# One kernel, two edits to its attention stages: float32 probabilities and values with two heads in column halves, and a second score pass in row halves

## The chip, the cores and the metric

The kernel runs on one core of a Trainium2 chip. The metric is the device time of one execution in microseconds; the time shown for a kernel is the median of its runs. TensorE multiplies, VectorE, ScalarE and GpSimd (POOL in the profile) do the elementwise work, SyncE's queue issues most transfers. TensorE's results land in PSUM, eight banks of 512 float32 columns over 128 partitions.

## What is computed

Two blocks over 1024 tokens of width 1024, all inputs and outputs in float32. The first block has two layers (a Hyena convolution mixer, then grouped-query attention), each with a cross attention to 256 memory rows and a mixture of experts; the second has a recurrent layer beside a latent attention (MLA), and a state-space layer. The change touches the three attentions only:

```python
# memory cross attention, 4 heads of 64, in both layers of the first block; and blocked_gqa: 12 query heads, 4 key heads of 64
s = einsum(q, k) / 8 ;  p = softmax(s) ;  out = einsum(p, v)
# _mla_attention: 8 heads, scores over 64 + 32 columns, values of 64, causal in blocks of queries
s = (einsum('bqhd,bkhd->bhqk', q_nope, k_nope) + einsum('bqhr,bkr->bhqk', q_rope, k_rope)) * scale
p = softmax(where(mask, s, -inf)) ;  out = einsum('bhqk,bkhd->bqhd', p, v)
```

## The kernel before

Precision is kept by splitting: a float32 operand becomes a rounded part ("hi", type fp32r, which TensorE multiplies in one pass) and the remainder ("lo", also fp32r). `Kern.split` (L130, L134) writes hi on ScalarE and lo on VectorE or POOL. A projection uses three of the four products (`mm3`).

GQA (`Gqa.attend`, L1414). Heads run one after the other. `keys` makes for a key head two tiles of 128 partitions and 1024 columns: hi twice, one above the other, and lo twice. `stack` makes for a query head one tile with hi in one half of the partitions and lo in the other (its lower half on POOL, L1411); its pool has two buffers. So one matmul over 128 rows adds two products, and `scores` (L840) needs two passes of 1024 columns per tile of 128 queries: against hi, then against lo. `exp_rows` takes the row maximum out of PSUM (VectorE, L873) and the exponential with its sum (ScalarE, L875). `pT` (L885) transposes the 128x1024 probabilities in eight blocks (TensorE, L125), four to a bank, and splits them into `gph` and `gpl`; in one of eight cases the split is done later on POOL (`pc`). After four such tiles (half of the queries), `out_heads` (L903) multiplies: the 128 weight columns are the values' hi and lo side by side, the moving operand is `gph`, then `gpl`, for each of eight key blocks; the two halves of the 128 output partitions are taken out by ScalarE and added by POOL, the reciprocal sums are brought into rows by four transposes (`columns_to_rows`) and multiplied in on POOL, and the result goes to DRAM. Of PSUM's eight banks the score tiles have 2 x 2 (`s`), the transposes 3 (`tp`), the output 1 (`ov`).

Memory attention (`Mem.attend`, L814) is the same on 256 keys with two heads in one score tile; its calls are issued between the projections of the two mixers. MLA (`mla_attend`, L1709) runs eight heads over tiles t = 4, 5, 6, 7, 0, 1, 2, 3; `mla_tile` makes scores in three passes in up to two of four one-bank tiles, `mla_pT` transposes and splits, `mla_out` multiplies, scales by the sums and a gate tile loaded from DRAM, and stores. Its probability tiles have one buffer each, for one head.

The order of the instructions on each engine isn't written out by hand. It is fixed when the kernel is built (`schedule_with_timeline_sim=True`): for each engine, as soon as it is free in a model of the run, the ready instruction that stands earliest in the program is taken. On the chip each engine then runs its list in order.

## Time and profile before

| | us |
|---|---|
| median of 3 runs | 3917.97 (3914.57 to 3920.28) |
| profiled execution | 3916.14 |
| its span in the trace | 3913.2 |
| first attention's own stage (GQA) | 1615 to 1920 of the span |
| last attention (MLA) | 2812 to 2978 |
| memory attention | within 90 to 440, and within 1500 to 1615 |

How to read the rows below: times are microseconds from the start of the span, means are ns. PE is TensorE, PEld its weight loads, DVE VectorE, ACT ScalarE. A tile is named by the program (`gs` GQA's scores, `prob` probabilities, `pT` their transposes, `ov` the product with the values; `as`, `apT`, `ao` the same in MLA; `ms` the memory's scores), a line is that of the helper that issued it. Matmuls are pipelined: the distance of two starts is what one costs in a row, its own duration is longer.

### The profile page before, as it was taken

The page shows a single profiled execution, that of the slowest core. Times are in us where ns is not written, and L with a number is a line of the kernel's source. Part 1 is how long each engine was busy: PE and PEld are TensorE (multiplying, and loading weights), DVE is VectorE, ACT ScalarE, POOL GpSimd, SP SyncE. Part 2 cuts the span into 40 slices and gives each one's busy share as a digit, 9 for nine tenths or more (in the row PEclk, how much of TensorE's full clock was granted, in tenths as well). Part 3 has the DMA queues.
Part 4 walks back from the last instruction along what each step waited for, and adds up shares of the span by engine and source line. Part 5 has one row for each costly group of instructions (what it writes and reads, how often), then busy time and mean ns, then how long its engine had stood idle before and what let it go on. Part 6 is the DMA issues. An engine that isn't in the chain of part 4 may idle for free.

```text
span 3913.2 us, 52413 instructions
## 1 busy us (share of the span) xinstructions
PE 3553.0 (91%) x19471; PEld 3025.0 (77%) x19471; DVE 2859.2 (73%) x4803; ACT 2030.9 (52%) x3047; POOL 1453.8 (37%) x1175
## 2 busy tenths in 40 slices
PE   7997999985999979899877999989998999999998
PEld 6885878764988879777767888878777877778777
DVE  6547878867988789677687988766476666665675
ACT  4433532223776754799625776645584245545430
POOL 2004745400543422244302444313451049774610
PEclk9998999897999999999988999999999999999999
DMA  4223333464999951000366999841014312222241
GB/s 159 91 82 108 116 130 116 138 212 173 363 366 346 369 166 37 11 12 12 115 242 228 386 348 345 302 136 53 33 48 131 100 48 92 71 76 85 90 171 65
DMA packets 205720, 603.61 MB, mean 154 GB/s; under 512 B 23110, under 2 KB 114104, under 8 KB 179865
## 3 DMA queue, kind: packets, MB, share of 16 engines
q1 hardware_dynamic: 193769, 558.58, 39.4%
q0 software_dynamic: 11696, 41.69, 4.1%
q8 instruction: 153, 2.51, 0.3%
q14 instruction: 102, 0.84, 0.1%
HBM read 503.60 MB, written 96.60 MB: 153 GB/s over the span
## 4 chain that ended last, share of the span: by engine, by line
PE 54%; DVE 11%; POOL 7%; ACT 4%; DMA 3%; issue 3%; SPq 0%; ACTq 0%; DVEq 0%; POOLq 0%
PE out L176 11%; PE gate L176 8%; PE xbc L176 5%; PE up L176 5%; PE down L176 4%; DVE mwl L134 4%; PE ov L176 2%; PE gs L176 2%; PE pT L125 2%; PE z L176 2%; PE as L176 1%; POOL csr L2062 1%; PE qk L176 1%; PE xr L176 1%; POOL csr L2061 1%
## 5 line engine op out<-in xcount | busy, mean ns | idle before, releaser
L134 DVE TENSOR_TENSOR mwl<-mwr,mwh 128x1024 fp32r<-128x1024 f32 x486 | 646.5, 1382 | 55.2 <-ACT mwh L130 54.3
L130 ACT ACTIVATE mwh<-mwr 128x1024 fp32r<-128x1024 f32 x576 | 563.0, 1051 | 52.5 <-PE up L176 28.8
L134 POOL TENSOR_TENSOR mwl<-mwr,mwh 128x1024 fp32r<-128x1024 f32 x90 | 257.4, 2885 | 272.2 <-ACT mwh L130 253.8
L1226 POOL DMA_INDIRECT xg<-xn_d,idx x32 | 58.8, 1838 | 466.2 <-DVE gsc L1224 465.6
L915 POOL TENSOR_TENSOR oh<-oh,oh 64x256 f32<-64x256 f32 (+1 forms) x56 | 56.0, 1000 | 396.3 <-ACT oh L914 392.1
L134 DVE TENSOR_TENSOR gpl<-pT,gph 128x512 fp32r<-128x512 f32 x168 | 110.6, 685 | 40.6 <-ACT gph L130 26.7
L1494 DVE SCALAR_TENSOR_TENSOR cv<-xbc,sdcols,cv 128x1021 f32<-128x1021 f32 (+2 forms) x72 | 91.9, 1276 | 65.3 <-ACT cv L1491 65.0
L125 PE MATMUL pT<-ident,prob 128*128 128x128 f32 x896 | 127.0, 277 | 13.6 <-DVE gpl L134 8.6
L873 DVE TENSOR_REDUCE mx<-gs 128x1 f32<-128x1024 f32 x96 | 116.9, 1218 | 30.6 <-PE gs L176 30.4
L176 PE MATMUL gate<-mwh,xgl 128*128 128x384 f32 x512 | 137.3, 349 | 0.5 <-DVE xgl L134 0.4
L125 PEld LDWEIGHTS pT<-ident,prob 128*128 128x128 f32 x896 | 106.0, 142 | 39.2 <-DVE gpl L134 6.3
L176 PE MATMUL gate<-mwl,xgh 128*128 128x384 f32 x512 | 134.6, 342 | 0.9 <-DVE mwl L134 0.8
L176 PE MATMUL gate<-mwh,xgh 128*128 128x384 f32 x512 | 134.0, 341 | 0.0
L176 PE MATMUL up<-mwl,xgh 128*128 128x384 f32 x512 | 132.0, 337 | 1.9 <-DVE mwl L134 1.9
L176 PE MATMUL out<-pwh,pyl 128*128 128x512 f32 x384 | 122.4, 400 | 11.4 <-DVE pyl L134 5.9
L176 PE MATMUL up<-mwh,xgh 128*128 128x384 f32 x512 | 132.1, 338 | 0.0
L176 PE MATMUL up<-mwh,xgl 128*128 128x384 f32 x512 | 131.6, 337 | 0.0
L130 ACT ACTIVATE xgh<-xgT 128x512 fp32r<-128x512 f32 (+1 forms) x68 | 38.1, 567 | 173.2 <-PE xgT L125 172.6
L176 PE MATMUL down<-mwl,hh 128*128 128x512 f32 x384 | 122.2, 399 | 6.1 <-POOL mwl L134 6.0
L134 DVE TENSOR_TENSOR wl<-raw,wh 128x1024 fp32r<-128x1024 f32 x71 | 109.2, 1539 | 22.6 <-ACT wh L130 22.5
L176 PE MATMUL down<-mwh,hl 128*128 128x512 f32 x384 | 122.1, 397 | 0.0
L176 PE MATMUL out<-pwh,pyh 128*128 128x512 f32 x384 | 121.2, 396 | 0.0
(753 smaller groups left out, 11725.7 us busy)
## 6 DMA issues: line engine op xcount, KB each, us to landing
mwr<-in_exp_w_gate_dram SPq DMA_DIRECT2D x64, 1536.0 KB
mwr<-in_exp_w_up_dram SPq DMA_DIRECT2D x64, 1536.0 KB
mwr<-in_exp_w_down_dram SPq DMA_DIRECT2D x64, 1536.0 KB
csr<-cs_d SPq DMA_DIRECT2D x32, 512.0 KB
raw<-in_ssd_w_in_dram SPq DMA_DIRECT2D x15, 1024.0 KB
k_d<-kev SPq DMA_DIRECT2D x54, 256.0 KB
kt<-k_d SPq DMA_DIRECT2D x54, 256.0 KB
raw<-in_hy_w_in_dram SPq DMA_DIRECT2D x10, 1024.0 KB
```

Of the source, the lines that this page charges most:

```text
L125: self.nc.tensor.transpose(out, in_, self.ident[:n, :n])
L130: nc.scalar.activation(out=hi, in_=src, func=AF.Copy)
L134: e.tensor_tensor(out=lo, in0=src, in1=hi.bitcast(F32), op=OP.subtract)
L176: self.nc.tensor.matmul(out=out, lhsT=lhsT, rhs=rhs, start=start, stop=stop)
L873: nc.vector.tensor_reduce(out=mx, in_=ps, axis=AX.X, op=OP.max, negate=True)
L915: nc.gpsimd.tensor_tensor(out=o2, in0=o2, in1=o, op=OP.add)
L1226: nc.gpsimd.indirect_dma_start(out=xg, out_offset=None, in_=self.xnD, in_offset=bass.IndirectOffsetOnAxis(ap=idx[:, 0:1], axis=0))
L1494: nc.vector.scalar_tensor_tensor(out=out[:, d:T], in0=ps[:, 0:T - d], scalar=cols[j], in1=out[:, d:T], op0=OP.mult, op1=OP.add)
L2061: G.tensor_tensor(out=m, in0=m, in1=per(self.cs[:, c, hs], P), op=OP.subtract)
L2062: G.tensor_tensor(out=m, in0=m, in1=self.msk.rearrange("p (o l) -> p o l", o=1).broadcast_to([P, 8, P]), op=OP.mult)
```

## The change

Values and probabilities stay float32. `pT` copies each bank of transposes once, to a float32 tile, by the engine that its argument names: in GQA the first four blocks by ScalarE, the last four by VectorE; in the memory attention all by ScalarE; in MLA the first bank by VectorE, the second by ScalarE. `out_pair` multiplies for two heads: head 0 writes output partitions 0 to 63, head 1 partitions 64 to 127, in turn, each with 64 weight columns (its float32 values). GQA and MLA therefore go by pairs of heads. `pair_rows` spreads the pair's reciprocal sums over 2 x 64 columns on POOL and transposes them once for both heads; the product is one VectorE instruction over 128 partitions, and one store goes out per pair. `pair_scores` makes GQA's scores for a pair: head 0's full pass against hi, then lo for both heads in row halves (64 partitions each, query hi against key lo; the product of query lo and key lo falls away), then head 1's full pass. The PSUM banks stay as they were.

```diff
@@ -814,8 +814,7 @@
     def attend(self, wk, mixT, row0, pair, qs, tg, pk=None):
         K = self.K
-        ph = wk.tile([P, 4, 256], F32R, name="mph", tag="mph")
-        pl = wk.tile([P, 4, 256], F32R, name="mpl", tag="mpl")
+        pt = wk.tile([P, 4, 256], F32, name="mpt", tag="mpt")
         for tt in range(2):
             t = tg * 2 + tt
             ps = K.psum("ms", "s")
@@ -823,11 +822,13 @@
                 h = 2 * pair + q
                 scores(K, ps[:, q * 256:(q + 1) * 256], qs[q][:, t * P:(t + 1) * P], self.k2[h], self.kl2[h])
             prob = softmax_rows(K, pk or wk, ps[:, 0:512], 2)
-            pT(K, prob, ph, pl, tt)
...
+            pT(K, prob, pt, tt, ("act",))
+        r0 = row0 + pair * P
+        ps = out_pair(K, [[pt[:, 2 * q + mb] for mb in range(2)] for q in range(2)],
+                      [[self.v[:, mb, (2 * pair + q) * 64:(2 * pair + q + 1) * 64] for mb in range(2)] for q in range(2)], "tp")
+        o = wk.tile([P, 256], F32, name="oh", tag="oh")
+        K.nc.scalar.activation(out=o, in_=ps[:, 0:256], func=AF.Copy)
+        K.nc.sync.dma_start(out=mixT.piece(r0, r0 + P, tg * 256, (tg + 1) * 256), in_=o)
 def query_stack(K, s, ps, q):
@@ -876,13 +877,37 @@
     return p
-def columns_to_rows(K, ps, v):
...
+def pair_scores(K, ps, qs, kk):
+
+
+    n = ps[0].shape[1]
+    cuts = [slice(o, min(n, o + 512)) for o in range(0, n, 512)]
+    own = [slice(0, 64), slice(64, 128)]
+    for c in cuts:
+        K.mm(ps[0][:, c], qs[0], kk[0][0][:, c], True, False)
+    for c in cuts:
+        for q in range(2):
+            K.mm(ps[q][:, c], qs[q][own[q]], kk[q][1][own[q], c], q == 1, q == 0)
+    for c in cuts:
+        K.mm(ps[1][:, c], qs[1], kk[1][0][:, c], False, True)
+
+
+def pair_rows(K, pool, sums, tag):
+
+    nc = K.nc
+    n = sums.shape[1]
+    nc.vector.reciprocal(out=sums, in_=sums)
+    b = pool.tile([P, n, 2, 64], F32, name=tag + "b", tag=tag + "b", bufs=1)
+    nc.gpsimd.tensor_copy(out=b, in_=sums.rearrange("p n (q o) -> p n q o", o=1).broadcast_to([P, n, 2, 64]))
+    rp = K.psum("rT", "tp")
+    for j in range(n):
+        K.transpose(rp[:, j * P:(j + 1) * P], b[:, j].rearrange("p q d -> p (q d)"))
+    r = pool.tile([P, n * P], F32, name=tag, tag=tag)
+    nc.scalar.activation(out=r, in_=rp[:, 0:n * P], func=AF.Copy)
+    return r
+
+
+def pT(K, prob, pt, tt, engs):
     nc = K.nc
     s = slice(tt * P, (tt + 1) * P)
@@ -891,36 +916,22 @@
         for k in range(4):
             K.transpose(ps[:, k * P:(k + 1) * P], prob[:, (h + k) * P:(h + k + 1) * P])
         v = ps[:, 0:512].rearrange("p (k t) -> p k t", k=4)
-        if h in off:
...
+        if engs[h // 4] == "act":
+            nc.scalar.activation(out=pt[:, h:h + 4, s], in_=v, func=AF.Copy)
         else:
-            K.split(ph[:, h:h + 4, s], pl[:, h:h + 4, s], v)
...
+            nc.vector.tensor_copy(out=pt[:, h:h + 4, s], in_=v)
+
+
+def out_pair(K, pt, vs, tag, cut=lambda k: 0):
+
+    n = pt[0][0].shape[1]
     ps = K.psum("ov", tag)
-    for j, (k, v) in enumerate(kv):
...
+    m = len(pt[0])
+    for k in range(m):
+        c = cut(k)
+        for q in range(2):
+            K.mm(ps[q * 64:(q + 1) * 64, c:n], vs[q][k], pt[q][k][:, c:n], k == 0, k == m - 1)
+    return ps
 NE = 16
@@ -1373,8 +1384,7 @@
         for j, (wh, wl) in enumerate(ws):
             K.mm3(ps[:, j * 256:(j + 1) * 256], lambda k: uh[:, k, ts], lambda k: ul[:, k, ts], lambda k: wh[:, k], lambda k: wl[:, k], KT, n=256)
         if u == 1:
-            p3 = ps[:, 0:256].rearrange("p (h d) -> p h d", h=4)
-            K.split(self.v[:, t, :, 0:64], self.v[:, t, :, 64:128], p3)
+            nc.scalar.activation(out=self.v[:, t], in_=ps[:, 0:256], func=AF.Copy)
             return
         x = self.rotated(wk, ps, u, t)
         tp = K.psum("qkT")
@@ -1413,23 +1423,29 @@
     def attend(self, wk, mixT, kpools, qp, op):
         K = self.K
-        for h in range(NH):
-            kv = h // 3
...
+        kk = {}
+        for pr in range(NH // 2):
+            hs = (2 * pr, 2 * pr + 1)
+            for h in hs:
+                if h // 3 not in kk:
+                    kk[h // 3] = self.keys(kpools[h // 3 % 2], h // 3)
+            qs = [self.stack(qp, h) for h in hs]
             for tg in range(2):
-                ph = wk.tile([P, 8, 512], F32R, name="gph", tag="gph")
-                pl = wk.tile([P, 8, 512], F32R, name="gpl", tag="gpl")
...
+                pt = [wk.tile([P, 8, 512], F32, name=f"gpt{q}", tag=f"gpt{q}") for q in range(2)]
+                sm = op.tile([P, 4, 2], F32, name="gsm", tag="gsm", bufs=2)
                 for tt in range(4):
                     t = tg * 4 + tt
-                    ps = K.psum("gs", "s")
-                    scores(K, ps, qs[:, t * P:(t + 1) * P], k2, kl)
...
+                    ps = [K.psum("gs", "s") for q in range(2)]
+                    pair_scores(K, ps, [s[:, t * P:(t + 1) * P] for s in qs], [kk[h // 3] for h in hs])
+                    for q in range(2):
+                        prob = exp_rows(K, wk, ps[q], sm[:, tt, q:q + 1])
+                        pT(K, prob, pt[q], tt, ("act", "dve"))
+                po = out_pair(K, [[pt[q][:, kb] for kb in range(8)] for q in range(2)],
+                              [[self.v[:, kb, h // 3 * 64:h // 3 * 64 + 64] for kb in range(8)] for h in hs], "ov")
+                r = pair_rows(K, op, sm, "orc")
+                o = op.tile([P, 512], F32, name="oh", tag="oh")
+                K.nc.vector.tensor_tensor(out=o, in0=po[:, 0:512], in1=r, op=OP.mult)
+                K.nc.sync.dma_start(out=mixT.piece(pr * P, (pr + 1) * P, tg * 512, (tg + 1) * 512), in_=o)
 ALPHA = float(np.float32(4.0 ** 0.25))
@@ -1694,7 +1710,7 @@
             v = ps.rearrange("p (h d) -> p h d", h=8)
             nc.scalar.activation(out=kf[:, :, 0:64], in_=v[:, :, 0:64], func=AF.Copy)
             nc.gpsimd.tensor_copy(out=kf[:, :, 64:96], in_=self.kr[:, t:t + 1].broadcast_to([P, 8, 32]))
-            K.split(self.v[:, t, :, 0:64], self.v[:, t, :, 64:128], v[:, :, 64:128])
+            nc.vector.tensor_copy(out=self.v[:, t], in_=v[:, :, 64:128])
             for src, dst, eng in ((qf, self.qT, "act"), (kf, self.kT, "dve")):
                 for h0 in range(0, 8, 4):
                     tp = K.psum("mT", "tp")
@@ -1720,19 +1736,19 @@
             for s in (slice(0, T),) if h else (slice(0, 512), slice(512, T)):
                 for i, x in ((2, self.kT), (0, self.qT)):
                     K.split(qk[i][:, s], qk[i + 1][:, s], x[h // 4][0:96, h % 4, s], lo_eng="pool" if h else "dve")
-            pp = []
...
+            q = h % 2
+            if q == 0:
+                pp = [[cp.tile([P, 4 + 4 * tg, 512], F32, name=f"ap{x}{tg}") for tg in range(2)] for x in range(2)]
+                sm = cp.tile([P, 2, NT, 2], F32, name="asm", tag="asm", bufs=2)
+                G.memset(sm[:, 1, 0:4], 0.0)
             todo = [4, 4]
             for t in (4, 5, 6, 7, 0, 1, 2, 3):
-                p = self.mla_tile(wk, qk, t, idb, msk, sm)
...
+                p = self.mla_tile(wk, qk, t, idb, msk, sm[:, :, :, q])
+                tg = t // 4
+                self.mla_pT(p, pp[q][tg], t)
+                todo[tg] -= 1
+                if q and not todo[tg]:
+                    self.mla_out(wk, yT, h // 2, tg, [x[tg] for x in pp], sm[:, :, 4 * tg:4 * tg + 4])
     def mla_tile(self, wk, qk, t, idb, msk, sm):
@@ -1761,42 +1777,36 @@
             nc.scalar.activation(out=p[:, o:o + w], in_=ps[:, 0:w], func=AF.Exp, bias=mx[:, 2 * m - 2:2 * m - 1], accum_out=sm[:, j, t:t + 1])
         return p
-    def mla_pT(self, p, pp, t):
...
+    def mla_pT(self, p, pt, t):
+
+        K, nc = self.K, self.K.nc
         cs = slice(t % 4 * P, (t % 4 + 1) * P)
         for k0 in range(0, t + 1, 4):
             m = min(4, t + 1 - k0)
             tp = K.psum("apT", "tp")
             for k in range(m):
                 K.transpose(tp[:, k * P:(k + 1) * P], p[:, (k0 + k) * P:(k0 + k + 1) * P])
-            K.split(ph[:, k0:k0 + m, cs], pl[:, k0:k0 + m, cs], tp[:, 0:m * P].rearrange("p (k t) -> p k t", t=P))
...
+            src = tp[:, 0:m * P].rearrange("p (k t) -> p k t", t=P)
+            if k0:
+                nc.scalar.activation(out=pt[:, k0:k0 + m, cs], in_=src, func=AF.Copy)
+            else:
+                nc.vector.tensor_copy(out=pt[:, k0:k0 + m, cs], in_=src)
+
+    def mla_out(self, wk, yT, pr, tg, pt, sm):
         K, nc = self.K, self.K.nc
-        gt = wk.tile([64, 512], F32, name="ag", tag="ag", bufs=1)
...
+        gt = wk.tile([P, 512], F32, name="ag", tag="ag", bufs=1)
+        dst = yT.piece(512 + pr * P, 512 + (pr + 1) * P, tg * 512, (tg + 1) * 512)
         nc.sync.dma_start(out=gt, in_=dst)
-        rs = K.small.tile([P, 4], F32, name="ars", tag="ars", bufs=2)
+        rs = wk.tile([P, 4, 2], F32, name="ars", tag="ars", bufs=2)
         nc.vector.tensor_tensor(out=rs, in0=sm[:, 0], in1=sm[:, 1], op=OP.add)
-        nc.vector.reciprocal(out=rs, in_=rs)
...
+        r = pair_rows(K, wk, rs, "arb")
         nc.gpsimd.tensor_tensor(out=gt, in0=r, in1=gt, op=OP.mult)
-        po = K.psum("ao", "ov")
...
+        n = tg * 4 + 4
+        po = out_pair(K, [[x[:, k] for k in range(n)] for x in pt], [[self.v[:, k, 2 * pr + q] for k in range(n)] for q in range(2)], "ov",
+                      lambda k: max(0, k - tg * 4) * P)
+        o = wk.tile([P, 512], F32, name="aoh", tag="aoh", bufs=1)
+        nc.vector.tensor_tensor(out=o, in0=po[:, 0:512], in1=gt, op=OP.mult)
         nc.sync.dma_start(out=dst, in_=o)
```

The allocations change with it: `mv`, `vst`, `mlv` hold 64 float32 columns per head (`mlv` now `[P, NT, 8, 64]`).

## Rows read from the trace of the kernel before

**Rows 1.** The page: busy time, share of the span and instructions of TensorE.

```profile
PE 3553.0 (91%) x19471; PEld 3025.0 (77%) x19471; DVE 2859.2 (73%) x4803; ACT 2030.9 (52%) x3047; POOL 1453.8 (37%) x1175
```

**Rows 2.** Busy times by stretch: memory attention twice, GQA, MLA; last columns clock, DMA.

```profile
core 0: us, PE busy (x) PEld busy (x) DVE busy (x) ACT busy (x) POOL busy (x), PEclk, DMA share, GB/s
90.00:440.00 350.00, 324.88 (x1564) 265.20 (x1563) 225.85 (x287) 144.37 (x267) 92.09 (x120) 0.95 0.28 95
...
1500.00:1615.00 115.00, 107.67 (x864) 104.08 (x863) 95.86 (x266) 64.21 (x154) 26.93 (x25) 0.98 0.09 25
1615.00:1920.00 305.00, 288.86 (x1637) 236.33 (x1636) 225.18 (x295) 265.74 (x480) 129.86 (x109) 0.98 0.07 17
...
2812.00:2978.00 166.00, 144.71 (x896) 118.37 (x896) 126.39 (x282) 135.91 (x348) 83.06 (x54) 0.94 0.19 53
```

**Rows 3.** Groups by form, 1615 to 1921 us: busy us, mean ns | idle before.

```profile
L873 DVE TENSOR_REDUCE mx<-gs 128x1 f32<-128x1024 f32 x96 | 116.9, 1218 | 30.6 <-PE gs L176 30.4
L134 DVE TENSOR_TENSOR gpl<-pT,gph 128x512 fp32r<-128x512 f32 x168 | 110.6, 685 | 40.6 <-ACT gph L130 26.7 <-issue 12.0
L125 PE MATMUL pT<-ident,prob 128*128 128x128 f32 x768 | 107.8, 278 | 13.6 <-DVE gpl L134 8.6 <-ACT prob L875 5.0
...
L130 ACT ACTIVATE gph<-pT 128x512 fp32r<-128x512 f32 x168 | 93.6, 595 | 17.5 <-PE pT L125 16.5
...
L1411 POOL TENSOR_TENSOR gqs<-qT,gqs 64x1024 fp32r<-64x1024 f32 x10 | 23.8, 2378 | 34.1 <-ACT gqs L1410 34.0
```

**Rows 4.** Order of time on TensorE in GQA: start us, us, what.

```profile
1753.64 1.03 PE L125 MATMUL pT<-ident,prob 128*128 128x128 f32 x8
...
1757.28 0.63 PE L176 MATMUL gs<-gkl,gqs 128*128 128x512 f32 x2
1757.74 0.60 PE L125 MATMUL rT<-ident,gsm 128*64 128x128 f32 x4
1758.10 0.48 PE L176 MATMUL ov<-gph,vst 128*128 128x512 f32 x1
...
1759.82 0.39 PE L176 MATMUL ov<-gpl,vst 128*128 128x512 f32 x1
1760.06 0.60 PE L125 MATMUL pT<-ident,prob 128*128 128x128 f32 x4
```

**Rows 5.** Order of time on TensorE in the state-space scan.

```profile
3303.57 0.39 PE L176 MATMUL z<-uh,wl 128*128 128x512 f32 x1
3303.89 1.09 PE L176 MATMUL yd<-csr,xf 128*64 128x128 f32 x16
3304.91 0.50 PE L176 MATMUL st<-xdh,bl 128*128 128x512 f32 x1
```

**Rows 6.** Groups by form on TensorE, whole span: float32 with 64 weight columns.

```profile
L176 PE MATMUL yd<-csr,xf 128*64 128x128 f32 x512 | 37.0, 284 | 4.1 <-POOL xf L2067 4.0
...
L176 PE MATMUL mlp<-ft,w 33*64 33x512 f32 x4 | 1.9, 602 | 0.0
```

**Rows 7.** Groups by form, 2765 to 2812 us: a VectorE copy out of PSUM.

```profile
L1707 DVE COPY mkT<-mT 96x512 f32<-96x512 f32 x16 | 10.3, 676 | 0.4 <-PE mT L125 0.4
```

**Rows 8.** Order of time on ScalarE in GQA: one exponential and its sum.

```profile
1757.77 1.16 ACT L875 ACTIVATE prob<-gs,mx 128x1024 f32<-128x1024 f32 x1
1758.77 0.25 ACT L875 ACTIVATION_READ_ACCUMULATOR prob<-gs,mx 128x1 f32 x1
```

**Rows 9.** Order of time on VectorE in GQA; in brackets the idle time before.

```profile
1761.38 0.69 DVE L134 TENSOR_TENSOR gpl<-pT,gph 128x512 fp32r<-128x512 f32 x1 [1.49 <-issue]
```

**Rows 10.** Order of time on TensorE behind two gaps in GQA.

```profile
1621.54 1.97 PE L125 MATMUL pT<-ident,prob 128*128 128x128 f32 x8 [3.23 <-ACT prob L875]
...
1770.65 1.62 PE L125 MATMUL pT<-ident,prob 128*128 128x128 f32 x7 [1.98 <-DVE gpl L134]
```

**Rows 11.** Busy times by stretch: behind the first gap, and one head of MLA.

```profile
1621.00:1624.00 3.00, 2.46 (x10) 2.37 (x11) 0.68 (x1) 2.63 (x6) 0.00 (x0) 0.50 0.09 22
...
2870.00:2887.60 17.60, 16.78 (x113) 14.16 (x112) 14.13 (x35) 15.68 (x43) 9.88 (x8) 1.00 0.13 32
```

More of the change, by code (lines that the diff above doesn't have):

```diff
@@ L876, in exp_rows @@
     return p
-def columns_to_rows(K, ps, v):
-    for j in range(v.shape[1]):
-        K.transpose(ps[0:64, j * P:(j + 1) * P], v[:, j:j + 1].broadcast_to([P, 64]))
-def pT(K, prob, ph, pl, tt, pool=None, off=()):
+def pair_scores(K, ps, qs, kk):
[22 more added lines that the diff above has]
+def pT(K, prob, pt, tt, engs):
     nc = K.nc
@@ L1415, in attend @@
         K = self.K
-        for h in range(NH):
-            kv = h // 3
-            if h % 3 == 0:
-                k2, kl = self.keys(kpools[kv % 2], kv)
-            qs = self.stack(qp, h)
+        kk = {}
[5 more added lines that the diff above has]
+            qs = [self.stack(qp, h) for h in hs]
             for tg in range(2):
-                ph = wk.tile([P, 8, 512], F32R, name="gph", tag="gph")
-                pl = wk.tile([P, 8, 512], F32R, name="gpl", tag="gpl")
-                sm = K.small.tile([P, 4], F32, name="gsm", tag="gsm", bufs=2)
+                pt = [wk.tile([P, 8, 512], F32, name=f"gpt{q}", tag=f"gpt{q}") for q in range(2)]
+                sm = op.tile([P, 4, 2], F32, name="gsm", tag="gsm", bufs=2)
                 for tt in range(4):
                     t = tg * 4 + tt
-                    ps = K.psum("gs", "s")
-                    scores(K, ps, qs[:, t * P:(t + 1) * P], k2, kl)
-                    prob = exp_rows(K, wk, ps, sm[:, tt:tt + 1])
-                    pT(K, prob, ph, pl, tt, wk, (4,) if tt == 2 else ())
-                out_heads(K, op, ph, pl, [(kb, self.v[:, kb, kv]) for kb in range(8)],
-                          mixT.piece(h * 64, h * 64 + 64, tg * 512, (tg + 1) * 512), tag="ov", sums=sm)
+                    ps = [K.psum("gs", "s") for q in range(2)]
[9 more added lines that the diff above has]
+                K.nc.sync.dma_start(out=mixT.piece(pr * P, (pr + 1) * P, tg * 512, (tg + 1) * 512), in_=o)
 ALPHA = float(np.float32(4.0 ** 0.25))
```

62 lines of the change are left out of this document (5 added, 57 removed).

## The prediction

> **What bounds the kernel now.** I read the page's busy shares first [rows 1]: TensorE is busy for 91% of the span, so a change to attention pays only where it shortens what TensorE does or waits for. Then the busy times by stage [rows 2], for the four stretches in which an edited function runs. In the first attention block's own stage (GQA: 12 query heads, 4 key heads, 1615 to 1920 us) TensorE is busy 289 of 305 us and ScalarE 266: two engines are nearly full. In the last attention (MLA, 2812 to 2978) TensorE has 145 of 166 us. The memory attention runs inside projections (90 to 440 and 1500 to 1615 us), with TensorE busy 93 to 94%. The groups of instructions of the GQA stretch [rows 3] give the prices, and TensorE's order of time [rows 4] shows the rhythm.
>
> My unit for GQA is one pair of heads with one half of the queries (four tiles of 128 query rows per head): 12 such units fill the 305 us, so 25.4 us each. TensorE issues per unit: 32 score matmuls 0.23 us apart (two in 0.46, [rows 4]), 7.4 us; 64 transposes at (1.03 - 0.28) / 7 = 0.107 us [rows 3, 4], 6.9; 32 value matmuls 0.24 apart [rows 4], 7.6; 8 transposes of the sums at 0.09, 0.7. Together 22.6 of 25.4 us: TensorE binds, with 11% of gaps.
>
> **What the change does to TensorE's work in GQA.**
> - Values. Each block of keys had two one-pass matmuls per head; now each head has a float32 one. The trace records a float32 matmul as two instructions of two passes: with 512 columns and 64 weight columns they come (1.9 - 0.602) / 3 = 0.43 us apart when alone [rows 6]. Do column halves run at once? The state-space scan does just that with 128 columns: 16 instructions in 1.09 us, or (1.09 - 0.28) / 15 = 0.054 us each, where a full-width float32 transpose of as many columns takes 0.107 [rows 3 to 6]. So they do, and 32 instructions cost 32 x 0.43 / 2 = 6.9 us for 7.6 before: nearly nothing is won here. Alone they would cost 13.8.
> - Scores. Half of the second pass goes: 16 full matmuls (3.7 us) and 16 in row halves. No row of the trace has two row halves at once; the bounds are half price (1.9 us) and full price (3.7). I take 1.9, after the nearest row, the column halves.
> - Transposes of probabilities stay, 6.9; those of the sums are halved, 0.4.
> Sum: 19.8 us (21.6 without row halves at once) for 22.6.
>
> **Off TensorE.** Per unit ScalarE gets 8 copies in place of 14 roundings and 2 deferred copies of the same size (0.6 us each, [rows 3]), and loses all four evictions of the output; VectorE's 14 subtractions of 0.685 become 8 copies at about 0.68 (nearest row: 96x512 out of PSUM, [rows 7]) and one product. POOL loses two sums, two products and two deferred splits and gets one copy of 128x512, between nothing and 2.4 us (its dearest row, 64x1024 with two inputs, [rows 3]); the value matmuls run meanwhile. These engines get room. If TensorE kept its 11% of gaps, a unit would take 22.2 us, and GQA gain 38 us.
>
> **Why I don't forecast that.** The score banks are two tiles, before and after. Before, each holds one head's tile and each goes its own way. Afterwards a pair takes both, and the row-half pass writes both, so it needs both freed: the next tile of queries starts only when the second exponential of this one has ended. Follow the ring from that moment, all from [rows 3, 4, 8]. The second head's 8 transposes come first, being earlier in the program and released by the same exponential: 0.86. Row halves, two at a time: 0.46, and 0.16 for the tail of a matmul (0.62 for two, less 0.46). Maximum of head 0, then of head 1 on the same VectorE: 2 x 1.22. Exponential of head 1 with its read: 1.25 (1757.77 to 1759.02). Sum 5.2 us, of which TensorE works 0.46 + 0.46 + 0.46 + 2 x 0.86 = 3.1; its first score pass and head 0's transposes fit into the wait. Four rings are 20.8 us, already more than the 19.8 of work.
>
> The value matmuls could fill these gaps only if they were spread over the rings. But the order of an engine is fixed at build time, earliest in program first among what is ready. In the trace the value matmuls of a unit run as a block: eight of them from 1758.10 to 1760.06, though an exponential had ended at 1759.02 and its transposes were ready [rows 4, 8]; VectorE then stood idle 1.49 us before 1761.38 [rows 9]. With the change the block is 6.9 us, half of it released by ScalarE's copy of the last tile (0.43 for four transposes, 0.17 tail, 0.6 copy: 1.2 us into the ring), the rest by VectorE's soon after. The next unit's scores end only at 0.86 + 0.92 = 1.8 us: the row halves fit before the block, more or less, head 1's full pass doesn't. So head 1's maximum and exponential wait for the block, nothing overlaps with it, and a unit takes 4 x 5.2 + 6.9 + 0.4 = 28.1 us: 2.7 us more than now, x 12 = +32 us. If that full pass gets in front of the block, the exponentials hide under it and about 2 us come back: 26.1 us, +8 us in all. I take the first, by 1.2 against 1.8 us.
>
> Two smaller terms. The stacked queries have two buffers: one head in use and one ahead before, the pair after. A new pair's stack (ScalarE, then 2.4 us on POOL, [rows 3]) thus starts only after the last scores of the old one; ring and POOL run side by side, so I take 1 us at each of 5 changes (0 to 2.4), +5. And the clock: after 3.23 us and after 1.98 us without work TensorE came back at half rate (8 transposes in 1.97 us, 7 in 1.62, against 8 in 1.03), and was granted 0.50 for the 3 us from 1621 [rows 4, 10, 11]. A ring has one gap of 5.2 - 3.1 = 2.1 us. At half rate a ring grows by 0.86 + 0.46 = 1.3 us. Between none and all 36 rings outside the blocks that is 0 to 47 us; I take a fifth, +10.
>
> **The other places.** In MLA a head takes 17.6 us and TensorE is busy 16.8 of them [rows 11]. Scores and transposes stay; half of the sums' transposes go (4 x 0.09), and the values get a little cheaper if GQA's 7.6 to 6.9 holds here. I take -0.8 per head, -6 in all. There the score banks are not paired, so no ring arises; the block of values is at most 5.6 us (13/16 of GQA's columns), beside four small tiles whose scores are ready. Relief of ScalarE and VectorE at the stage's unsteady ends may give up to -15; bunching of the values into every second head up to +5. Memory attention and MLA's projection: TensorE is full there [rows 2], the removed splits lie beside it: -3 (0 to -6).
>
> **Sum.** The profiled execution took 3916.1 us (span 3913.2), 1.8 below the median of the three runs, 3918.0. 3916.1 + 32 + 5 + 10 - 6 - 3 = 3954, and 3956 on the scale of the median.
>
> A rule speaks against the change too. The trace: going into the scan's column halves costs 0.32 us instead of 0.23, and the first matmul behind takes 0.50 [rows 5]; but a matmul behind transposes takes 0.48 as well [rows 4]. The Trainium skill, "TensorEngine Tiling (Array Packing)", Tiling Modes, says that changing the tiling mode, not just the tile, drains TensorE. By that each row-half pass pays on both sides, 48 x 2 x 0.1 = some 10 us more if all lay in the ring, an estimate from these rows; by my reading nothing new. The sum goes without it.
>
> **Rivals.**
> - Gaps get filled (faster). If the build spreads the values over the rings, or the first exponentials of a unit overlap more than I see, a unit falls to the ring's 20.8 to 22.2 us: -38 to -55 us, less clock loss, with 5 - 9 from the rest: 3859 to 3880. For: ScalarE and VectorE get much room. Against: the block in [rows 4]. It decides from the point at which a unit takes under 25.4 us. Chance 0.35.
> - The scores slip in front of the block (26.1 us), the clock holds: 3916 + 8 + 5 - 9 + 2 = 3922. Chance 0.13, on either side of no change.
> - The clock stays low in the rings: up to 3990. Chance 0.10.
> - Halves don't run at once. Row halves: +0.5 us in each ring, +22 us, 3978; column halves at 512 columns: 12 x 6.9 = +83 us, 4039. Chance 0.07. The rows of the scan speak against the second.
> - My forecast, 3935 to 3975: chance 0.35.
>
> **How the numbers follow.** The measurement tells some 0.2% (8 us) from no change. Faster has the first rival, 0.35, and 0.02 of the second; same the rest of the second less 0.03, so 0.08; slower everything else, 0.55. Range, eight in ten: from the filled gaps, 3862, to the low clock, 3990. My forecast's own range is 3935 to 3975.
>
> **What would show it.** Right: in the GQA stretch VectorE's maxima come in pairs some 5 us apart, TensorE waits for "ACT prob" at each tile, and 16 to 32 value matmuls stand in a row with VectorE idle beside them; the stretch is over 320 us long, TensorE's busy time in it lower than 289, ScalarE's below 220. Wrong: value matmuls in pieces between the tiles' transposes, a stretch of 270 us or less, or the clock below 0.9 throughout. Pairs of value instructions should start 0.22 us apart on average; 0.43 would deny the column halves, and 0.23 for each row half the row halves.

## The result: 3964 us, 1.1% slower

The changed kernel takes 3964.07 us (median of 4 runs, 3961.18 to 3964.92) beside 3919.12 for the kernel before (3914.57 to 3923.05) in the same comparison: a ratio of 1.0108, 95% interval 1.0096 to 1.0121. The forecast was 3956, its own case 3935 to 3975.

The profiled execution took 3964.92 us, its span is 3962.9. The time is in GQA: from its first to its last score instruction 334.0 us pass (1625.6 to 1959.6), before 292.1 (1615.5 to 1907.6); to the last value instruction it is 344.9, before 303.1. The busy times by stretch, GQA and then MLA (columns as in [rows 2]):

```profile
core 0: us, PE busy (x) PEld busy (x) DVE busy (x) ACT busy (x) POOL busy (x), PEclk, DMA share, GB/s
1625.60:1972.00 346.40, 322.11 (x1585) 176.39 (x1585) 196.00 (x225) 193.25 (x325) 33.98 (x26) 0.98 0.04 14
2865.00:3031.00 166.00, 149.82 (x872) 101.99 (x873) 106.94 (x229) 98.78 (x262) 54.43 (x34) 0.96 0.16 50
```

ScalarE, VectorE and POOL are relieved as the diff promises (266 to 193, 225 to 196 and 130 to 34 us, [rows 2]). TensorE isn't: 322 us where it had 289. Relief of three engines bought nothing, because the fourth binds. The clock granted is 0.98, as before. The groups by form of the same stretch:

```profile
L874 DVE TENSOR_REDUCE mx<-gs 128x1 f32<-128x1024 f32 x96 | 116.4, 1222 | 51.9 <-PE gs L176 48.0 <-ACT prob L876 2.1 <-ACT gpt L920 0.7
L125 PE MATMUL pT<-ident,prob 128*128 128x128 f32 x768 | 108.7, 283 | 21.1 <-ACT prob L876 20.6
L176 PE MATMUL ov<-gpt,vst 128*64 128x512 f32 x384 | 97.8, 598 | 1.8 <-ACT gpt L920 1.8
L176 PE MATMUL gs<-gk,gqs 128*128 128x512 f32 x192 | 72.2, 458 | 2.7 <-DVE gqs L1421 2.7
L176 PE MATMUL gs<-gkl,gqs 64*128 64x512 f32 x192 | 66.3, 456 | 1.3 <-ACT prob L876 1.3
L922 DVE COPY gpt<-pT 128x512 f32<-128x512 f32 x96 | 65.5, 685 | 14.4 <-PE pT L125 13.0
```

The row halves (`gkl`, 64 rows) keep TensorE busy for 66.3 us; the full passes that they replace had 61.7 for the same count of 192. The order of time on TensorE shows the rest (start, us; in brackets the idle time before). First the values of one unit, with VectorE's next instruction among them, then one ring, with two of its weight loads (PEld):

```profile
1741.42 4.50 PE L176 MATMUL ov<-gpt,vst 128*64 128x512 f32 x18
1745.86 0.66 PE L125 MATMUL rT<-ident,orcb 128*128 128x128 f32 x4
1746.45 3.65 PE L176 MATMUL ov<-gpt,vst 128*64 128x512 f32 x14
1750.03 1.10 PE L125 MATMUL pT<-ident,prob 128*128 128x128 f32 x8
1750.19 0.69 DVE L1447 TENSOR_TENSOR oh<-ov,orc 128x512 f32<-128x512 f32 x1 [7.43 <-PE ov L176]
...
1760.48 1.09 PE L125 MATMUL pT<-ident,prob 128*128 128x128 f32 x8 [0.26 <-ACT prob L876]
1761.33 0.71 PE L176 MATMUL gs<-gk,gqs 128*128 128x512 f32 x2
1761.97 0.29 PEld L176 LDWEIGHTS gs<-gkl,gqs 64*128 64x128 f32 x2 [0.37 <-issue]
1761.98 0.73 PE L176 MATMUL gs<-gkl,gqs 64*128 64x512 f32 x2
1762.63 0.42 PEld L125 LDWEIGHTS pT<-ident,prob 128*128 128x128 f32 x4 [0.36 <-ACT prob L876]
1762.64 0.66 PE L125 MATMUL pT<-ident,prob 128*128 128x128 f32 x4
1763.22 0.73 PE L176 MATMUL gs<-gkl,gqs 64*128 64x512 f32 x2
1763.88 0.73 PE L176 MATMUL gs<-gk,gqs 128*128 128x512 f32 x2
1764.45 0.60 PE L125 MATMUL pT<-ident,prob 128*128 128x128 f32 x4
1765.39 1.09 PE L125 MATMUL pT<-ident,prob 128*128 128x128 f32 x8 [0.34 <-ACT prob L876]
```

Three things are to be seen. The 32 value instructions stand in one block of 8.6 us (1741.42 to 1750.03), beside which VectorE waits 7.43 us: that is what the forecast said. (In five of the twelve units 30 of the 32 stand in a row, in seven 18 and 14 with a few instructions between.) The row halves of the two heads do not stand together: the build issued head 0's two, four transposes, then head 1's two, because head 1's score tile comes free later (the exponentials that free the two tiles end at 1760.3 and 1762.3). So each head goes its own way, as before, and no pair has to be free at once: that is not what the forecast said. And a ring (1760.48 to 1765.39) is 4.9 us, nearly all of it TensorE at work: it waits 0.34 us. The unit that begins there ends 28.5 us after the one before (the sums' transposes start at 1745.86 and 1774.33); 28.1 was forecast. The units differ, though: the sums' transposes follow each other at 22.0 to 34.1 us, and the average, 345.5 us for twelve units, is 28.8.

### The profile page after: what moved, and what is told of

It is laid out like the page before. It is cut to its first block, busy times and chain, and to the rows that moved or that the text cites. A ratio compares the mean times of both kernels' runs of the same rounds, so it can differ in the third digit from the quotient of the medians.

```text
span 3962.9 us, 51447 instructions
## 1 busy us (share of the span) xinstructions
PE 3599.9 (91%) x19391; PEld 2945.0 (74%) x19391; DVE 2782.9 (70%) x4631; ACT 1896.6 (48%) x2747; POOL 1292.3 (33%) x1039
## 4 chain that ended last, share of the span: by engine, by line
PE 55%; DVE 11%; POOL 6%; ACT 4%; DMA 3%; issue 2%; SPq 0%; ACTq 0%; DVEq 0%; POOLq 0%
PE out L176 10%; PE gate L176 8%; PE xbc L176 5%; PE up L176 5%; DVE mwl L134 4%; PE down L176 4%; PE ov L176 4%; PE qk L176 2%; PE gs L176 2%; PE pT L125 2%; PE z L176 2%; PE as L176 1%; POOL csr L2072 1%; PE xr L176 1%; ACT prob L876 1%
## 5 line engine op out<-in xcount | busy, mean ns | idle before, releaser
L125 PE MATMUL pT<-ident,prob 128*128 128x128 f32 x896 | 128.2, 281 | 21.1 <-ACT prob L876 20.6
L125 PEld LDWEIGHTS pT<-ident,prob 128*128 128x128 f32 x896 | 101.7, 143 | 60.5 <-ACT prob L876 42.7
L134 DVE TENSOR_TENSOR wl<-raw,wh 128x1024 fp32r<-128x1024 f32 x71 | 113.0, 1592 | 22.9 <-ACT wh L130 22.8
L876 ACT ACTIVATE prob<-gs,mx 128x1024 f32<-128x1024 f32 x96 | 106.8, 1113 | 37.6 <-DVE mx L874 35.7
L176 PE MATMUL out<-pwl,pyh 128*128 128x512 f32 x384 | 121.1, 396 | 0.0
L176 PE MATMUL xbc<-ul,wh 128*128 128x512 f32 x368 | 120.4, 404 | 0.0
```

The lines of the kernel that those rows point to most:

```text
L125: self.nc.tensor.transpose(out, in_, self.ident[:n, :n])
L134: e.tensor_tensor(out=lo, in0=src, in1=hi.bitcast(F32), op=OP.subtract)
L176: self.nc.tensor.matmul(out=out, lhsT=lhsT, rhs=rhs, start=start, stop=stop)
L876: nc.scalar.activation(out=p, in_=ps, func=AF.Exp, bias=mx, accum_out=sm)
```

## Three theories

- A, the forecast: the pair moves in step, and the ring of the two heads (maxima and exponentials one behind the other) sets the time.
- B: each head has its own ring; what costs is the bare block of values, and a ring that grew a little.
- C: TensorE's own time binds, and it grew, because each turn between full passes and row halves costs something.

All times below are compared with runs of the kernel before on the same chip (3920.8 to 3921.7 us). "GQA" is the time from its first score to its last value instruction, and TensorE's busy time is taken over the same stretch up to that instruction's end; "experts" runs from the last value instruction to the first projection of the second block.

| kernel | us | ratio (95%) | GQA | TensorE busy in GQA's stretch | experts |
|---|---|---|---|---|---|
| before (again, e6) | 3918.6 | 0.9997 (0.9987 to 1.0007) | 302.4 | 287 of 303 | 650.7 |
| changed (again, e5) | 3965.5 | 1.012 (1.0104 to 1.0135) | 345.1 | 321 of 346 | 653.1 |
| e1 scores by head | 3935.3 | 1.0035 (1.0023 to 1.0046) | 326.4 | 295 of 327 | 640.0 |
| e2 halves at once | 4013.1 | 1.0237 (1.0214 to 1.026) | 402.3 | 317 of 403, clock 0.89 | 640.2 |
| e3 by head, values spread | 3929.5 | 1.0021 (1.0012 to 1.0031) | 322.1 | 291 of 323 | 640.4 |
| e4 memory as before | 3944.4 | 1.0058 (1.004 to 1.0077) | 342.4 | 322 of 343 | 640.1 |
| e7 by head, spread in fixed order | 3892.6 | 0.9931 (0.9917 to 0.9945) | 289.5 | 282 of 290 | 640.2 |
| e8 GQA as before | 3914.9 | 0.998 (0.9971 to 0.9989) | 300.0 | 288 of 300 | 643.7 |
| e9 changed, spread in fixed order | 3920.5 | 0.9996 (0.9986 to 1.0006) | 310.1 | 305 of 311 | 643.5 |
| e10 halves at once, spread | 3929.2 | 1.0024 (1.0015 to 1.0034) | 312.5 | 281 of 313, clock 0.96 | 650.8 |
| e11 values apart (one run) | 4057.4 | | 416.1 | 395 of 417 | 649.8 |

The last column matters for the readings: no line of the experts' stage is edited anywhere, and yet it takes 640.0 to 643.7 us in e1 to e4 and e7 to e9, and 647.4 to 653.1 in both traces of the kernel before and of the changed one, in e10 and in e11. TensorE's order in that stage divides the kernels in the same way. By the tiles that they write and read, the experts' gate, up and down products come in one and the same order in the kernel before, the changed one, e10 and e11, and in another, the same for all, in the seven others; 44 of 2112 places hold another product. So an edit ahead changes the order that the build makes of what lies behind it, and with it go some 4 to 13 us. Not all of that is the order's: the two traces of the changed kernel, 647.4 and 653.1, differ by 6 by themselves. Conclusions on GQA are therefore drawn from the GQA column, not from the totals.

## The experiments

**e1: whole second pass, head by head.** It takes the row halves out and leaves the values as changed.

```diff
-                    pair_scores(K, ps, [s[:, t * P:(t + 1) * P] for s in qs], [kk[h // 3] for h in hs])
+                    for q in range(2):
+                        scores(K, ps[q], qs[q][:, t * P:(t + 1) * P], *kk[hs[q] // 3])
```

> The changed kernel, but each head's scores in two full passes as before (no row halves). In the changed kernel's trace a unit of GQA (two heads, four tiles) takes 28.5 us: four rings of 4.9 and a block of values of 8.6. Theory A (pairing, as predicted: a tile of queries waits until both score tiles are free): the pairing is gone, TensorE binds with some gaps, 24 us per unit, total -54 us against the changed kernel. Theory B (each head waits for its own score tile only; the ring grew because every step between full passes, row halves and transposes costs TensorE some 0.2 us more): ring 0.85 transposes + 1.0 scores + 0.2 + 1.22 maximum + 1.3 exponential = 4.6, total -13 us. Theory C (TensorE's own time, with those steps, binds in the ring too): 0.9 us less work per ring, total -42 us.

Measured: 3935.3 us, 29 below the changed kernel; 19 of them are GQA's (344.9 to 326.4), most of the rest the experts' order. A, with its 54, is refuted. TensorE's busy time falls by 27 us when whole passes take the place of half ones. The busy times of the stretch:

```profile
1627.30:1955.00 327.70, 295.25 (x1584) 185.45 (x1584) 194.86 (x225) 192.03 (x325) 33.93 (x26) 0.98 0.04 15
```

The order of time on TensorE tells why:

```profile
1810.19 0.71 PE L176 MATMUL gs<-gk,gqs 128*128 128x512 f32 x2
1810.51 0.42 PEld L176 LDWEIGHTS gs<-gkl,gqs 128*128 128x128 f32 x2
1810.74 0.63 PE L176 MATMUL gs<-gkl,gqs 128*128 128x512 f32 x2
1811.21 0.60 PE L125 MATMUL pT<-ident,prob 128*128 128x128 f32 x4
...
1814.08 0.63 PE L125 MATMUL pT<-ident,prob 128*128 128x128 f32 x4
1814.47 0.72 PE L176 MATMUL gs<-gk,gqs 128*128 128x512 f32 x2
1815.03 0.63 PE L176 MATMUL gs<-gkl,gqs 128*128 128x512 f32 x2
1815.50 0.60 PE L125 MATMUL pT<-ident,prob 128*128 128x128 f32 x4
```

From a full pass to the second pass 0.55 us, where the changed kernel had 0.65 (1761.33 to 1761.98); from there to the transposes 0.47, where it had 0.66. So a turn into row halves costs 0.10 and out of them 0.19 us: 0.29 for this pass. The other head's pass stands between four transposes and a full pass; these three together take 1.81 us in the changed kernel (1762.64 to 1764.45) and 1.42 here (1814.08 to 1815.50), 0.39 more. By the busy time the average is 27 / 96 = 0.28 for a pass. The rows also show where the time goes: here the weights of the second pass are loaded 0.23 us ahead of its matmuls (1810.51 for 1810.74), beside the pass before; the weights of the row halves only as their matmuls begin (1761.97 for 1761.98), and so are those of the transposes behind them (1762.63 for 1762.64). So it is throughout: the median lead of the second pass's first weights is 0.23 us in e1 and 0.00 in the changed kernel. Little came back for it, since two row halves of one head follow each other on the same rows, and the two heads' halves stand together in only 7 of 48 places of the changed kernel. B, with -13, is short of the measured -19, C with -42 over it.

**e2: the four row halves of a pair in a row.** Both full passes first, then the halves of head 1 and head 0 in turn, in a fixed order.

```diff
+    for q in range(2):
+        for c in cuts:
+            K.mm(ps[q][:, c], qs[q], kk[q][0][:, c], True, False)
...
     for c in cuts:
...
+        for q in (1, 0):
...
+                    st.enter_context(K.tc.issue_after(last))
+                last = K.nc.tensor.matmul(out=ps[q][:, c], lhsT=qs[q][own[q]], rhs=kk[q][1][own[q], c], start=False, stop=True)
```

> The changed kernel with the row-half pass moved behind both full passes and issued in the order head 1, head 0, head 1, head 0, so that two row halves can run at once; each then needs both score tiles. In the changed kernel the trace shows both halves of one head, then transposes, then those of the other. If row halves run at once, four should take some 0.5 us between steps, else 0.95. Theory A: nothing changes, as both tiles were waited for anyway (within 5 us of the changed kernel). Theory B: the pairing is real only here, ring 0.86 + 0.9 + 0.2 + 2 x 1.22 + 1.3 = 5.6, +30 us against the changed kernel. Theory C: less TensorE work per ring, -30 us.

Measured: 4013.1 us, GQA 57 us longer than in the changed kernel. The busy times of the stretch:

```profile
1619.80:2022.00 402.20, 316.62 (x1579) 187.83 (x1580) 192.68 (x222) 194.41 (x324) 35.07 (x23) 0.89 0.03 12
```

Two rings in TensorE's order of time:

```profile
1832.20 0.74 PE L894 MATMUL gs<-gkl,gqs 64*128 64x512 f32 x4
...
1837.94 0.73 PE L894 MATMUL gs<-gkl,gqs 64*128 64x512 f32 x4
1838.60 0.66 PE L125 MATMUL pT<-ident,prob 128*128 128x128 f32 x4
1841.29 1.97 PE L125 MATMUL pT<-ident,prob 128*128 128x128 f32 x8 [2.03 <-ACT prob L876]
1842.91 1.20 PE L176 MATMUL gs<-gk,gqs 128*128 128x512 f32 x2
...
1845.28 0.73 PE L894 MATMUL gs<-gkl,gqs 64*128 64x512 f32 x4
```

Four halves now take 0.66 us to the next start, as much as the changed kernel's two: row halves do run at once when their instructions alternate. But this is the pair in step that the forecast described. One ring is 5.74 us (5.2 forecast), and the next, in which TensorE came back from 2.03 us of waiting at half rate (8 transposes in 1.97 us), is 7.34; the forecast's price of a slow ring was 1.3 us more. The clock granted falls to 0.89 in the stretch. So A's mechanism and its clock loss are real, in a kernel that this change is not.

**e3: e1, with the values of a unit issued between the tiles of the next.**

```diff
+                    if pend:
+                        pend(2 * tt + 2)
```

`pend` issues the value instructions of the unit before, up to that key block: two blocks at each of the four tiles.

> Scores by head as in the first run of this call, and the value matmuls of a unit laid in the program between the tiles of the next unit, two key blocks behind each tile, instead of one block. All theories: the gaps of the rings get filled; TensorE then binds with 3.7 us of scores and transposes and 2.15 of values per tile: 24 us per unit, GQA 290 us, total 54 us under the changed kernel and 8 under the kernel before. If the block weren't what leaves the gaps, it would be as the first run.

Measured: 3929.5 us, GQA 4 us shorter than e1's. It was not the test that it was meant to be. The build decides where they go; TensorE's order of time:

```profile
1784.63 5.37 PE L176 MATMUL ov<-gpt,vst 128*64 128x512 f32 x24
```

24 of 32 instructions stand in one row here, 26 in most units. Likely because the output bank comes free only when the sums of the unit before have been brought into rows and multiplied in, which the list does late (here 1779.8 to 1782.8); what had been held back is then ready together.

**e4: the memory attention as in the kernel before**, all else as changed (its class and the helpers that it calls are the old ones).

> The changed kernel with the memory attention (its values, its transposes' splits, its output) as before; GQA and MLA changed. The changed kernel reaches GQA 10 us later than the kernel before. If the memory attention's edit costs that: GQA starts 10 us earlier, total -10 us. If it is the order that the build finds for the stages around it, which shifts with any edit: some other figure between 0 and -10, and the delay arises in stretches with no edited line.

Measured: 3944.4 us, 20 less than the changed kernel. It would be wrong to call these 20 the price of the memory edit: 13 of them are the experts' (653.1 to 640.1 us beside e5). The first memory score comes at 88.9 us instead of 93.0, as before (89.6); on the other hand, from the first instruction of the GQA projections (`qk`) to GQA's first score 187.5 us pass, as before (187.0), instead of 183.1. The edit costs some 4 us at the start and gives 4 back behind the second projection.

**e5 and e6: the changed kernel and the kernel before once more**, for stages on the same chip as e7 and e8.

> The changed kernel unaltered, beside the three others of this group, so that their stages can be compared on one chip. If what the edits outside GQA cost is theirs, GQA's first score matmul comes about 10 us later than in the kernel before run here, and the stage after GQA (last GQA score to the first matmul of the in-projection behind) is some 658 us as in the two first traces; if 658 against 651 us is the chip's, it is 651 to 653 here, for both kernels. Time about 3964.

> The kernel before, unaltered, for its stages on the same chip: about 3920 us in all. Landmarks of its first trace: first transform of Hyena 347.8 us, last 755.3; first GQA score 1615.5, last 1907.6; MLA's first score 2812.1, last 2962.6. If the 7 us that Hyena was longer in the changed kernel come from the edits, it keeps 407.5 us from first to last transform; if they come and go by themselves, it may as well be 414.

The changed kernel's profiled span is 44.5 us longer than the other's: 5.5 up to GQA's first score, 42.7 in GQA, 2.4 in the experts, -2.1 from there to MLA, -5.0 from MLA's first score to the last layer, 1.0 behind it. Hyena, from first to last transform, takes 407.5 and 410.0 us in the two traces of the kernel before, 414.3 and 411.2 in those of the changed one, 407.6 in e3 and 414.7 in e1, with one and the same order up to there: it varies by itself, and the 10 us that the first trace lost ahead of GQA were 5 in this one.

**e7: e1, with the values at fixed places**: behind the scores of the second, third and fourth tile of the next unit; and the sums brought into rows at once, so that the output bank comes free early.

```diff
+                    if pend:
+                        with K.tc.issue_after(getattr(last, "ins", last)):
+                            pend((0, 3, 6, 8)[tt])
...
+        po, at = [], [0]
+        r = pair_rows(K, op, sm, "orc")
```

`last` is the tile's last score instruction; `pend` issues the key blocks up to that number.

> The whole second pass for each head (as in e1), and the 32 value instructions of a unit placed behind the scores of the next unit's second, third and fourth tiles (12, 12 and 8) by a fixed order on TensorE, where the earlier spread had left 26 of 32 in one row. Ring theory (the block's 8.6 us are bare because nothing runs beside them): TensorE's 27 us of waiting for probabilities in e1 are filled, GQA falls from 328 to about 302 us, the kernel to about 3910. TensorE theory (its own 295 us bind): no more than half of that, GQA about 315, the kernel about 3922.

Measured: 3892.6 us, 0.9931 of the kernel before (0.9917 to 0.9945): faster than both kernels, though not all of it is GQA's (the experts are 10.5 us shorter than in e6). GQA takes 289.5 us, 13 less than in e6 and 37 less than in e1, the latter by nothing but the place of the 384 value instructions and of the sums' transposes. The busy times:

```profile
1619.83:1909.92 290.09, 282.16 (x1585) 182.50 (x1585) 195.14 (x222) 193.57 (x325) 33.25 (x23) 0.98 0.05 16
```

The values in TensorE's order of time:

```profile
1768.63 2.79 PE L176 MATMUL ov<-gpt,vst 128*64 128x512 f32 x12
1771.35 1.53 PE L125 MATMUL pT<-ident,prob 128*128 128x128 f32 x12
...
1774.67 2.79 PE L176 MATMUL ov<-gpt,vst 128*64 128x512 f32 x12
...
1781.17 1.94 PE L176 MATMUL ov<-gpt,vst 128*64 128x512 f32 x8
```

The transposes in the groups by form:

```profile
L125 PE MATMUL pT<-ident,prob 128*128 128x128 f32 x768 | 101.7, 278 | 5.7 <-ACT prob L876 4.1 <-DVE gsm L899 1.2 <-DVE gpt L922 0.2
```

12, 12 and 8 of them, each while a maximum and an exponential run; TensorE's waits for probabilities fall from 27.3 us in e1 to 4.1, and a unit lasts 22.9 us in most places. This carries the part of B on the bare block: it was a loss of the whole chain, not of VectorE alone. GQA fell by more than B's 26 us: TensorE's idle time in the stretch shrank by 24 (32.4 to 7.9), its busy time by 13, and why the latter isn't shown.

**e8: GQA as before**, the edits of the memory attention and of MLA alone.

> GQA as in the kernel before; the edits of the memory attention and of MLA alone. The forecast's terms for them: -6 and -3, so about 3911 us. By the first traces: +5 at the start (first memory scores and values), -4 behind the second projection, -4 in MLA: about 3917. If the edits ahead of GQA cost 10 us as in the first trace: about 3926.

Measured: 3914.9 us, 0.998 (0.9971 to 0.9989). Set against it, the GQA edit costs 3965.5 - 3914.9 = 51 us, of which, by the profiled executions, GQA's stage has 45 (345.1 to 300.0) and the experts' 9. The forecast's terms were -9 for the other edits (measured -7) and 32 + 5 + 10 = 47 for GQA. But the -7 is no clean proof of those terms: MLA gives 4.3 (440.6 us from its first score to the last layer, for 444.9), the experts' other order 7, and the profiled execution of e8, at 3919.1 the longest of its eleven, has lost 12 us ahead of GQA again.

**e9: the changed kernel, only the values at fixed places as in e7.** The row halves stay.

> The changed kernel with the score passes as it has them (row halves, head by head as the build orders them) and only the value instructions placed as in e7. Against e7 it tells what the row halves cost once the block is gone; against the changed kernel what the block cost. If each turn into a row-half pass and out of it costs TensorE what e1 showed (322 against 295 us busy, 27 us in GQA), GQA is 288 + 27 = 315 us and the kernel about 3920. If TensorE's waits hid the turns, GQA stays near 288 us and the kernel near 3893.

Measured: 3920.5 us, GQA 310.1: 35 less than the changed kernel, 20.6 more than e7. TensorE is busy 305.2 us of the stretch, 23 more than in e7: the turns cost nearly as much without the block as the 27 us with it (e1). The busy times:

```profile
1628.48:1939.14 310.66, 305.15 (x1585) 169.10 (x1585) 194.98 (x222) 194.34 (x325) 33.28 (x23) 0.98 0.04 15
```

TensorE's order of time:

```profile
1760.45 0.73 PE L176 MATMUL gs<-gkl,gqs 64*128 64x512 f32 x2
1761.11 0.73 PE L891 MATMUL gs<-gk,gqs 128*128 128x512 f32 x2
...
1766.43 0.73 PE L176 MATMUL gs<-gkl,gqs 64*128 64x512 f32 x4
1767.09 0.73 PE L891 MATMUL gs<-gk,gqs 128*128 128x512 f32 x2
```

Two halves and four halves both take 0.66 us to the next start: in 12 places of this kernel the build happened to put the two heads' halves together, so that 84 passes pay for turns instead of 96.

**e10: e2's halves at once and e7's places.**

> Row halves of both heads alternately, so that they run at once (as in e2), and the values placed as in e7. In e2 the pair of heads moved in step and TensorE stood idle and at half clock in each ring. Forecast's ring theory: a ring of 5.2 us with 12 value instructions inside its wait, so 4 x 5.2 = 20.8 us a unit plus turns, GQA 255 to 270 us, the kernel 3860 to 3880. If a coupled ring is longer than that because the exponentials of both heads queue up (e2 showed 6 to 7 us in places), a unit is 25 us or more, GQA over 300 us, the kernel 3905 or slower.

Measured: 3929.2 us, GQA 312.5. The values fill the gaps in part, TensorE's work is less than in e9 (281 us busy, for 305), and yet the stretch is no shorter: the pair in step binds. Of TensorE's 32 us without work, 7.7 are waits for the pair's query stacks on POOL (0.8 in e9). One ring, TensorE and ScalarE in order of time:

```profile
1764.21 0.74 PE L894 MATMUL gs<-gkl,gqs 64*128 64x512 f32 x4
1764.88 2.80 PE L176 MATMUL ov<-gpt,vst 128*64 128x512 f32 x12
1766.37 1.11 ACT L876 ACTIVATE prob<-gs,mx 128x1024 f32<-128x1024 f32 x1 [2.41 <-DVE mx L874]
1768.35 1.12 ACT L876 ACTIVATE prob<-gs,mx 128x1024 f32<-128x1024 f32 x1 [0.77 <-PE pT L125]
...
1770.44 0.73 PE L894 MATMUL gs<-gkl,gqs 64*128 64x512 f32 x4
```

This ring is 6.23 us, others 5.8. The second exponential waited 0.77 us for transposes (they free its probability buffer), and these stood behind the value instructions. The forecast's 20.8 us for a unit with filled gaps was too good: a unit takes 22 to 28.5 us, in most places 25.

**e11: the values of one head before those of the other**, in all three attentions, so that no two column halves stand side by side.

```diff
-    for k in range(m):
-        c = cut(k)
-        for q in range(2):
+    for q in range(2):
+        for k in range(m):
+            c = cut(k)
```

> The changed kernel with the values of one head before those of the other, in GQA, MLA and the memory attention, so that no two column halves stand side by side on TensorE. If column halves do run at once, value instructions now start 0.43 us apart in place of 0.23, and GQA's 384 cost up to 12 x 6.9 = 83 us more, less what falls into waits: 4010 to 4060. If they never did, the time stays near 3964.

Measured: 4057.4 us, 92 more than the changed kernel; GQA 71 more, MLA 25 more between its first and last score. A head's values in TensorE's order of time:

```profile
1762.54 7.08 PE L176 MATMUL ov<-gpt,vst 128*64 128x512 f32 x16
```

All of GQA's in the groups by form:

```profile
L176 PE MATMUL ov<-gpt,vst 128*64 128x512 f32 x384 | 167.0, 604 | 0.0
```

TensorE is busy with them for 167.0 us instead of 97.8. 16 instructions in 7.08 us are (7.08 - 0.60) / 15 = 0.43 apart; in the changed kernel 18 in 4.50, (4.50 - 0.59) / 17 = 0.23. Column halves run at once at 512 columns too.

## Why the forecast was near, and where it was wrong

The number came out 8 us low and within the range of its own case, but that it came so near is luck: errors of opposite sign make it up. In GQA 32 + 5 + 10 = 47 us were forecast and 42 came. Of these the 15 for stacks and clock were not found, and the units were longer than forecast, 28.8 us on the average for 28.1, though their rings were shorter. Outside GQA -9 was forecast, and some +3 came. Step by step:

- **"With the change the block is 6.9 us ... nothing overlaps with it": right**, and the largest effect. The block with its turns and the sums' transposes is 8.6 us, not 7.3. Its placing is worth 35 us (e9) to 37 us (e7) of GQA. The block itself was an inference: before, the values of such a unit ran in pieces of at most 9 instructions ([rows 4] show one of 8), but for one row of 16 at the stage's end.
- **Column halves at 0.22 us each: right** (0.23; e11).
- **"Afterwards a pair takes both, and the row-half pass writes both, so it needs both freed": failed.** The program lists the halves of both heads in one loop, but an instruction needs only its own tile, and the build puts each where that tile is free. A ring of one head is 4.9 us instead of 5.2. 4 x 5.2 + 7.3 = 28.1 and 4 x 4.9 + 8.6 = 28.2 are alike by chance.
- **"I take 1.9, after the nearest row, the column halves": failed**, as a consequence. The scan's rows [rows 5] showed halves that stand alternately in the program and in the list. In the changed kernel's list the halves of the two heads stand together in 7 of 48 places only, so nearly no row half runs beside another, and the full price of 3.7 us stayed.
- **"By my reading nothing new": failed, the costliest step.** The trace of before showed 0.32 and 0.50 us around the scan's halves; the runs show 0.10 us into row halves and 0.19 out of them, 0.29 to 0.39 for a pass, and in all 27 us of TensorE's time with the block (e1) and 23 without it (e9). The trace of before had a sign of such turns that the forecast passed over: its sum of TensorE's work, 22.6 us a unit or 271 for twelve, is 18 short of the 289 that [rows 2] show as busy. The Trainium skill, "TensorEngine Tiling (Array Packing)", Tiling Modes, says that a change of mode drains TensorE. The trace fits that, with weights that are loaded only as the halves begin; but from transposes to a full pass, both 128 by 128, it shows the same (in e1 two matmuls take 0.55 us there, 0.47 behind another full pass), so the change of mode isn't shown to be the only cause. The forecast's aside put 10 us on it, for 48 passes: the build had split nearly each in two.
- Hence **"TensorE's busy time in it lower than 289"** is wrong: 322. With the change TensorE has more to do, not less. Row halves were its only saving, and the values only break even.
- **Clock, +10: failed for this kernel** (0.98 before and after), since TensorE's waits for probabilities are under 0.5 us in 21 of 31 cases (the others are 1.1 to 2.4), where the forecast had 2.1 in each ring. Where the pair does move in step (e2), the clock falls to 0.89, and a ring with a slow stretch is 1.6 us longer (7.34 for 5.74).
- **Stacks, +5:** not tested by itself. TensorE's own wait for a stack is 2.7 us in all (the row `gs<-gk` above); in e10, where the pair moves in step, it is 7.7 us more.
- **MLA, -6:** measured -4.4 in the first pair of traces and -5.0 in e5 beside e6 (first score to the last layer). **Memory and projection, -3:** about nothing; 4 us lost at the start, which the forecast did not see, and 4 gained behind the second projection.
- **The fast rival** had its mechanism right: with the values between the tiles a unit takes 22.9 us, and GQA gets shorter than before. It gave 3859 to 3880; e7 takes 3893, with whole second passes. But the build doesn't do it by itself, not even when the program lists the values between the tiles (e3).

So B and C both hold, each for a part: e7 and e9 give the block 35 to 37 us, e1 and e9 give the turns 23 to 27 us of TensorE's time and 19 to 21 us of GQA's. A holds only for kernels that force the pair into step (e2, e10). Left open: why the experts' stage is 4 to 13 us faster in the other order, and what of e8's gain belongs to MLA.

## What to carry to other kernels

Two halves that could share the array did so here only where they stood next to each other in the engine's list: read the list that the build made, not the loop in the program, and count the turns between shapes (here 0.29 us or more for a pass of two halves, more than the half pass can save). While work of the bounding engine was gathered into one block at the end of a unit, the other engines' relief was worth nothing; placing the block's pieces behind the next unit's scores turned +1.1% into none with the change as it is, and into -0.7% with the row halves left out (10 to 13 us of each lie in the experts' stage). And judge an edit by its own stage: a build that orders by a model reorders stages behind it that nobody touched.

## What the hardware showed beyond the forecast

- The weights of a row half behind a full pass are loaded only as its matmuls begin (median lead 0.00 us in the changed kernel), those of a second full pass 0.23 us ahead of them (e1).
- Two row halves of one head take 0.66 us to the next start of another shape, and so do four of two heads (e9: 1760.45 to 1761.11 and 1766.43 to 1767.09).
- Column halves of float32 keep their pairing at 512 columns: 0.23 us an instruction, 0.43 when one half stands alone (e11).
- Three relieved engines (ScalarE -73, VectorE -29, POOL -96 us busy in GQA) left the stage 42 us longer.
